# Gram matrices and decays of the delta rule split off from the block substitution, in a Trainium2 kernel for one hybrid decoder layer

## The chip, the cores and the metric

The kernel runs on one core of one Trainium2 chip. The metric is the time of one execution on the device in microseconds (us), the median of the runs. In what follows PE is TensorE's matmul, PEld its weight load, DVE is VectorE, ACT is ScalarE, POOL is GpSimd, and SP is SyncE, which issues all of the kernel's DMAs. All of the core's engines take their instructions in the order in which they were written.

## What is computed

2048 tokens of width 1024, with 16 meta tokens ahead of them, go through one layer and a last RMSNorm. The reference, cut to what matters here:

```python
h = rmsnorm(x, norm_g)
p = h @ w_in                                  # 1024 x 8208
qkv, dn_z, dn_a, dn_b, sc_b, sc_c, sc_h, sc_z = split(p)
q, k, v = split(silu(causal_dwconv(qkv, width 4)))    # 8 heads x 128; q, k L2-normalised
g    = -exp(A_log) * softplus(dn_a + dt_bias);  beta = sigmoid(dn_b)
# gated delta rule, by chunks
g      = cumsum(g)
decay  = exp(where(causal, g_i - g_j, -inf))
a_low  = where(strict, beta * (k k^T) * decay, 0)
u, w   = solve(I + a_low, [v * beta, k * beta * exp(g)])
qk     = (q k^T) * decay
for each chunk:  v_new = u - w S;  o = (q exp(g)) S + qk v_new;  S = S exp(g_last) + k_dec^T v_new
o_dn = rmsnorm(o) * silu(dn_z)
o_sc = sc_b * causal_dwconv(sc_c * sc_h, width 3) * silu(sc_z)
out  = rmsnorm(x + concat(o_dn, o_sc) @ w_out)
```

## The kernel before

The tokens go in two halves of 1024. In the first phase each half runs 64 jobs, a job being the projection of one tile of 128 channels (`Job`, `run_group`): 3 groups of tokens by 24 matmuls, since each product is made of three float32r products of split operands (`hh`, `hl` are the high and low parts of the tokens, `wh`, `wl` those of the weights `wr`). Eight jobs belong to a head. Within a head they come as q, k, c, h, b, the gate sz of the short convolution, v, z, but for the first head of the first half and the last two of the second. Job j's weights are loaded by `load_w` into one of two `wr` buffers and split by ACT (`wh`) and DVE (`wl`). The second phase is the output projection, 48 matmuls a unit, and needs nothing of the last head until its eighth token tile.

The order of all engines but SP is written by the program itself. `Model` (line 30) follows the engines with costs of its own; the projections are cut into pieces of two or three matmuls, and after each piece `pump` (line 234) lets each of some streams (Python generators) take a step when the model's time has come to what it yielded. `require` (line 251) stops the projections, and lets only the streams go on, until a step is done: a head's k job waits for the scan of the head two before (`pre_k`, line 825), its v job for the transposes of the head before (`pre_v`, line 837, key `vr`).

The delta rule of the sixteen heads (8 heads, 2 halves) is four such streams, each going through the heads in order:

- `delta_front` (line 971): for head i the decays `E` (loaded as `gtd` rows, subtracted, masked by POOL, exp by ACT), then in four pieces the split keys and queries `kp` and six matmuls (the Gram matrices, `ta<-nb` in the profile, since `kp` takes the place of tile `nb`), which DVE turns into `M` (written over `E`) and `P`. The diagonal 32 x 32 blocks of `M` go to DRAM and back as `nb` (`nbd<-E`, `nb<-nbd`). On the first half `meta_inputs` handles the meta tokens. Then `substitution` inverts the blocks: 31 times a product (`prod<-nb,XT`) and a sum (`XT<-prod`) on DVE, row by row; `prod` starts as a copy of the constant `eyep`, made by POOL. The result goes to DRAM (`xtd<-XT`).
- `delta_back` (line 1108): the blocks come back as `W` (`W<-xtd`); six groups of four transposes bring k, v and q to token order (`ta<-ident,k` and so on); then `(I + M)^-1` of the whole chunks by small matmuls, the first of them `ta<-X,E`.
- `delta_scan` (line 1288): eight steps, one a chunk, each a chain PE `rec<-S,k`, DVE `yy`, PE `rec<-yy,W`, ACT `vn`, PE `rec<-vn,kd`, DVE `S`.
- `delta_out` (line 1338): norm, gate and store.

So `delta_front` starts the Gram pieces of head i + 1 only after the substitution of head i. The Gram pieces, `nb` and the prologue share the tile `nb`; the gate values use the tile `gw`. `normalize` (line 536) prepares the second half's tokens in between.

Of the kernel before, what the change touches and what calls it, by code (L numbers as in the profile page):

```python
# [12 lines left out]
ALU = mybir.AluOpType  # L13
# [16 lines left out]
class Model:  # L30
    """Time of each engine and of each tile, as work is issued; it decides the order of issue only."""
# [32 lines left out]
    def after(self, *aps, slot=None, eng=None, lag=0.0, least=0.02):  # L64
        """Time until the tiles are written, the slot is free and the engine is through but for lag."""
        t = self.free["PE"] + least
        for a in aps:
            t = max(t, self.ready.get(a.tensor.name, 0.0))
        if slot is not None:
            q = self.slots.get((id(slot[0]), slot[1]), ())  # L70
            if len(q) == self.bufs.get((id(slot[0]), slot[1])):
                t = max(t, self.used.get(q[0], 0.0))
        if eng is not None:
            t = max(t, self.free[eng] - lag)
        return t - self.free["PE"]
# [86 lines left out]
class Recorded:  # L162
    """The engines of a core, with all that they are given entered into the model."""
# [10 lines left out]
def hybrid_trunk(  # L174
# [41 lines left out]
    # ---- order of emission: a stream of projections, cut into pieces, and streams of dependent  # L216
    # steps that are issued between the pieces. `model` follows the engines as they are given work;
    # a step yields the time until what its successor needs is there.
# [28 lines left out]
    def when_done(fn, ap, most=100.0):  # L247
        """Issue fn once ap has been written."""
        timed.append((clk() + min(after(ap), most), fn))
# [46 lines left out]
    def newton(dst, a, y, t):  # L296
        """dst = y (1.5 - 0.5 a y^2): one Newton step for a ** -0.5 from y."""
        nc.vector.tensor_tensor(out=t, in0=y, in1=y, op=ALU.mult)
        nc.vector.scalar_tensor_tensor(t, t, -0.5, a, op0=ALU.mult, op1=ALU.mult)
        nc.vector.scalar_tensor_tensor(dst, t, 1.5, y, op0=ALU.add, op1=ALU.mult)  # L300
# [16 lines left out]
    # ---- constants of the first phase  # L317
# [12 lines left out]
    # eyep[32 q + block, m, i] = (i == 8 q + m)  # L330
    eyep = vt(pp, [128, 8, 32], "eyep")
# [10 lines left out]
    def constants():  # L342
        prow = vt(vp, [128, 128], "yy")
        nc.sync.dma_start(prow[0:96], dn_conv_w[0].rearrange("j (t p) -> (j t) p", p=128))
        nc.sync.dma_start(prow[96:120], sc_conv_w[0].rearrange("j (t p) -> (j t) p", p=128))
        nc.sync.dma_start(prow[120:121], dn_out_g)
        nc.sync.dma_start(negA, dn_A_log.partition_broadcast(128).rearrange("p o h -> p (o h)"))
        nc.sync.dma_start(dtb, dn_dt_bias.partition_broadcast(128).rearrange("p o h -> p (o h)"))
        wabr = vt(vp, [128, 128], "vn").rearrange("p (k c) -> p k c", c=16)
        nc.sync.dma_start(wabr, win[:, :, 4096:4112])  # L350
        while ("prologue", 0) not in done:
            yield 0.2
        yield after(prow, slot=(pta, "ta"))
        yield from hold()
        pt = ptile(pta, "ta", [128, 512])
        tr(pt[:, :121], prow[:121], 121)
        nc.vector.tensor_copy(pcol[:, :121], pt[:, :121])
        nc.gpsimd.memset(triu, 1.0)
        nc.gpsimd.affine_select(
            out=triu,  # L360
            in_=triu,
            pattern=[[1, 128]],
            compare_op=ALU.is_ge,
            fill=0.0,
            base=0,
            channel_multiplier=-1,
        )
        nc.gpsimd.memset(qcar, 0.0)
        nc.gpsimd.memset(ucar, 0.0)
        nc.gpsimd.memset(W, 0.0)  # L370
        nc.gpsimd.memset(X[0:64], 0.0)
        nc.gpsimd.memset(eyep, 0.0)
        for q in range(4):
            for m in range(8):
                nc.gpsimd.memset(eyep[32 * q : 32 * q + 32, m, 8 * q + m : 8 * q + m + 1], 1.0)
        nc.scalar.activation(negA, negA, AF.Exp)
        nc.vector.tensor_scalar(negA, negA, -1.0, None, op0=ALU.mult)
        nc.scalar.activation(wab[:, :, 0:16], wabr, AF.Copy)
        nc.vector.tensor_tensor(out=wab[:, :, 16:32], in0=wabr, in1=wab[:, :, 0:16], op=ALU.subtract)
        done.add("constants")  # L380
# [8 lines left out]
    def turn(hf, xt, k0, i, col, n, g):  # L389
        """Channels 4 k0 .. 4 k0 + 3 of a token tile into h^T."""  # L390
# [18 lines left out]
    def statistics(xt, n, jk):  # L409
        """mean square + eps and its approximate power -0.5."""  # L410
        ms, y = vt(vp, [128, 1], "pxm", bufs=3)[:n], vt(vp, [128, 1], "pxy", bufs=3)[:n]
        nc.scalar.activation(jk[:n, :D], xt, AF.Square, accum_out=ms)
        nc.gpsimd.tensor_scalar(ms, ms, 1.0 / D, EPS, op0=ALU.mult, op1=ALU.add)
        power(y, ms, 1, n)
        return ms, y

    def rootmean(xt, n):
        """(mean square + eps) ** -0.5 by ACT and GpSimd."""
# [14 lines left out]
    def prologue0():  # L433
        """h^T = (RMSNorm(x))^T of the first half as float32r parts hi + lo, [channel, k, token]
        by group."""
# [100 lines left out]
    def normalize(i):  # L536
        """RMSNorm of token tile i of the second half, to DRAM until the first half is through."""
        xt = vt(dp, [128, NC, 128], "kd").rearrange("p c i -> p (c i)")
        nc.sync.dma_start(xt, xs[HALF + 128 * i :][:128])
        yield after(xt)  # L540
        st = statistics(xt, 128, vt(dp, [128, 1840], "gw", dt=BF16))
# [48 lines left out]
    def hold(tag="ta", keep=False):  # L590
        """Wait until no step holds tag over several yields; or hold it."""
        while tag in held:
            yield 0.2
        if keep:
            held.add(tag)
# [3 lines left out]
    def gates(hf):  # L599
        """Token-major gate values [128, head, chunk]; on half 0 chunk 8 holds the meta tokens."""  # L600
# [21 lines left out]
        gw = vt(dp, [128, 920], "gw")  # L622
# [24 lines left out]
        # e = exp(-|a|), exp(-|b|), exp(min(b, 0))  # L647
# [11 lines left out]
        # log1p(e) = 2 atanh(s), s = e / (2 + e) <= 1 / 3  # L659
# [34 lines left out]
        nc.sync.dma_start(ged[hf, :Wd], gT[:Wd])  # L694
        G[hf] = dict(beta=beta, gcum=gcum, neg=neg, nch=nch)
# [3 lines left out]
    # ---- projections  # L699
# [76 lines left out]
    def conv_job(hf, s, col, t, pre, emit):  # L776
        """Projection, causal width-4 convolution and SiLU of channel tile t of q | k | v."""
# [43 lines left out]
    def slot_jobs(hf, s):  # L821
# [51 lines left out]
        # short convolution of channel tile s  # L873
# [67 lines left out]
    # ---- gated delta rule  # L941
    def substitution(nb, XT, prod):
        """Rows of (I + N)^-1 of unit lower triangular 32 x 32 blocks, a block and 8 columns per
        partition; nb[j, i] = N[i, j], XT[col, i], prod[col, i] = identity on entry."""
# [9 lines left out]
    def decay(hf, row0, n, E, gc):  # L954
        """E[j, c, i] = exp(g_i - g_j) for i >= j, else 0."""
# [14 lines left out]

    def delta_front():
        """Decays, the two triangular matrices, and the inverses of the diagonal blocks."""
        for i in range(2 * NH):
# [14 lines left out]
            )  # L988
            if hf == 0:
                Em = vt(dp, [NM, 1, NM], "mE")  # L990
# [20 lines left out]
            for c2 in range(4):  # L1011
                c0 = 2 * c2
                yield after(slot=(dp, "nb"))
                kp = vt(dp, [128, 2, 2, 2, 128], "nb", dt=F32R)
# [11 lines left out]
                for c in range(2):  # L1026
# [4 lines left out]
                    mmr(o_, lhsT=l_[:, :128], rhs=h_, start=False, stop=True)  # L1031
                yield after(pm, E)
# [27 lines left out]
            # inverses of the 32 x 32 diagonal blocks: partition 32 q + 8 b + c, columns 8 q .. 8 q + 7  # L1060
# [8 lines left out]
            if hf == 0:  # L1069
                yield from meta_inputs(hd, g_, d, Em)  # L1070
            yield after(nb)
# [12 lines left out]
            nc.gpsimd.tensor_copy(prod, eyep)  # L1084
# [20 lines left out]
            half[i] = dict(M=M, P=P, cd=cd, ir=ir, cj=cj)  # L1105
            done.add(("front", i))

    def delta_back():
        """The inverses of the whole chunks, and what the scan needs by token."""
        for i in range(2 * NH):  # L1110
# [11 lines left out]
            # q exp(g); token-major k, q norms, v  # L1122
# [41 lines left out]
            # (I + M)^-1 of the whole chunks from the blocks'  # L1164
# [52 lines left out]
    def meta_inputs(hd, g_, d, Em):  # L1217
        """The meta tokens' chunk: all but the inverse of its block."""
# [35 lines left out]
        def rows():  # L1254
            """One column of (I + N)^-1 per partition; entry 0 brings in the identity."""
# [82 lines left out]
    def delta_out():  # L1338
        """Norm, gate and store of the outputs."""
# [45 lines left out]
    # ---- output projection: weights of one column half as hi + lo parts, k by k  # L1385
# [9 lines left out]
    def first_wo():  # L1395
        """The first column half, into the place of the token groups that are through."""
# [28 lines left out]
    def load_mix(u, h):  # L1425
        """Half h of the mixed channels of unit u's tokens, in two float32r parts."""
# [18 lines left out]
    def unit_mm(u, nxt, same=None):  # L1445
        """One token tile by one column half; with `same`, the next unit takes over the mix."""
# [24 lines left out]
    # ---- first phase: all projections, the delta rule beside them  # L1471
# [21 lines left out]
    start(delta_front())  # L1493
    start(delta_back())
# [24 lines left out]
    # ---- second phase: output projection, residual, final norm  # L1519
# [117 lines left out]
```

## Time and profile before

| | |
|---|---|
| median of 3 runs | 2257.49 us (2250.55 to 2260.83) |
| span of the profiled execution, first to last instruction | 2248.0 us |
| its own time, by the median of the runs | some 9.5 us around the span |
| PE busy | 2175.4 us, 97% |
| DVE busy | 1456.6 us, 65% |
| ACT busy | 864.9 us, 38% |
| POOL busy | 153.3 us, 7% |
| mean granted clock of TensorE | 0.991 |

The execution that was profiled has no time listed of its own; its span and the 9.5 us to the median stand for it. The profile's page gives busy time by engine; the waits say which engine waited for what; the windows cut the span into stretches; the timelines list single instructions; the chain follows back from the last instruction to what released each. Matmuls overlap one another, so it is the time from start to start that tells the pace.

### The profile page before, as it was taken

To read this page: it belongs to the slowest core of one execution; us is meant where nothing else is said; L and a number is where in the kernel's file an instruction comes from. 1 tells how busy PE (TensorE), PEld (TensorE's weight loads), DVE (VectorE), ACT (ScalarE), POOL (GpSimd) and SP (SyncE) were. 2 spreads that over 40 slices of the span, in tenths; PEclk is the share of its full clock that TensorE was granted. 3 is DMA by queue.
4 is the path that set the end of the run, shared out by engine and by line. 5 is a ranking of instruction groups with operands and counts; after the bars stand their busy time and mean duration, and the time that the engine had idled before them with its cause. 6 is when DMAs were issued, how large, how long until landed. Compare 5 with 4: busy or idle time off the path is not lost.

```text
span 2248.0 us, 38710 instructions
## 1 busy us (share of the span) xinstructions
PE 2175.4 (97%) x15024; PEld 2061.8 (92%) x15024; DVE 1456.6 (65%) x4031; ACT 864.9 (38%) x2080; POOL 153.3 (7%) x312
## 2 busy tenths in 40 slices
PE   6999999999999999999999999999998799999998
PEld 6999999999999998999999999999998798888886
DVE  4676867676767767776868677676766465544322
ACT  5534434444444333443434343525352324422111
POOL 4000100000000000101000000000000000000000
PEclk9999999999999999999999999999999899999999
DMA  6444345443535677524343544253546664645321
GB/s 140 75 81 70 84 68 91 67 93 67 92 67 104 82 83 60 134 43 80 52 83 57 78 52 83 48 88 43 88 49 60 53 94 139 222 164 189 119 94 57
DMA packets 257237, 196.46 MB, mean 87 GB/s; under 512 B 62085, under 2 KB 226446, under 8 KB 257054
## 3 DMA queue, kind: packets, MB, share of 16 engines
q1 hardware_dynamic: 257054, 194.00, 47.5%
q8 instruction: 118, 1.93, 0.4%
q14 instruction: 65, 0.53, 0.1%
HBM read 157.89 MB, written 36.06 MB: 86 GB/s over the span
## 4 chain that ended last, share of the span: by engine, by line
PE 87%; DMA 6%; DVE 4%; SPq 1%; ACT 1%; issue 1%; POOL 0%; POOLq 0%; DVEq 0%; ACTq 0%
PE mm L118 74%; PE ta L118 7%; PE rec L118 4%; PE o L118 2%; SPq L118 1%; DMA nb<-nbd 1%; DMA wr<-in_w_in_dram 1%; DMA kd<-in_x_dram 1%; DVE prod L118 1%; DMA xtd<-XT 1%; DMA W<-xtd 1%; ACT junk L118 1%; DVE acc L118 1%; DVE XT L118 1%; DMA nbd<-E 0%
## 5 line engine op out<-in xcount | busy, mean ns | idle before, releaser
L118 PE MATMUL mm<-hh,wh 128*128 128x384 f32 (+3 forms) x3328 | 1043.6, 335 | 6.4 <-ACT hh L118 5.3
L118 PE MATMUL mm<-hl,wh 128*128 128x384 f32 (+3 forms) x3328 | 1015.1, 326 | 0.0
L118 PEld LDWEIGHTS mm<-hh,wh 128*128 128x128 f32 x3328 | 626.8, 189 | 21.0 <-ACT hh L118 5.9
L118 PEld LDWEIGHTS mm<-hl,wh 128*128 128x128 f32 x3328 | 627.3, 189 | 9.7
L118 PE MATMUL mm<-hh,wl 128*128 128x384 f32 (+3 forms) x3200 | 622.6, 327 | 2.8 <-DVE wl L118 2.8
L118 PEld LDWEIGHTS mm<-hh,wl 128*128 128x128 f32 x3200 | 512.6, 189 | 9.9 <-DVE wl L118 3.2
L118 DVE TENSOR_TENSOR wl<-wr,wh 128x512 fp32r<-128x512 f32 x348 | 233.8, 691 | 98.8 <-ACT wh L118 67.0
L118 DVE SCALAR_TENSOR_TENSOR acc<-raw,pcol,acc 128x384 f32<-128x384 f32 (+2 forms) x432 | 245.5, 573 | 60.5 <-ACT acc L118 55.9
L118 ACT ACTIVATE wh<-wr 128x1024 fp32r<-128x1024 f32 x178 | 187.8, 1055 | 79.3 <-PE mm L118 44.5
L118 DVE SCALAR_TENSOR_TENSOR prod<-nb,XT 128x8 f32<-128x8 f32 (+30 forms) x496 | 192.8, 389 | 39.1 <-DMA nb<-nbd 34.0
L118 DVE TENSOR_REDUCE XT<-prod 128x8 f32<-128x16 f32 (+30 forms) x496 | 147.2, 297 | 17.0
L118 ACT ACTIVATE raw<-mm 128x272 f32<-128x272 f32 (+2 forms) x144 | 65.7, 456 | 214.1 <-PE mm L118 214.1
L118 ACT ACTIVATE vn<-rec,cj 128x128 f32<-128x128 f32 x128 | 46.9, 366 | 252.0 <-PE rec L118 246.7
L118 ACT ACTIVATE sc_c<-mm 128x384 f32<-128x384 f32 (+4 forms) x99 | 45.0, 456 | 161.8 <-PE mm L118 158.0
L118 PE MATMUL mm<-oh,wh 128*128 128x512 f32 x256 | 101.9, 398 | 0.0
L118 PE MATMUL mm<-ol,wh 128*128 128x512 f32 x256 | 100.3, 392 | 0.0
L118 DVE TENSOR_TENSOR y<-mm,y 128x512 f32<-128x512 f32 x23 | 15.9, 692 | 110.7 <-PE mm L118 110.7
L118 DVE SCALAR_TENSOR_TENSOR yy<-rec,neg,vr 128x128 f32<-128x128 f32 x128 | 44.4, 347 | 62.3 <-PE rec L118 61.8
L118 ACT ACTIVATE ojk<-y 128x512 bf16<-128x512 f32 x23 | 14.5, 631 | 182.6 <-DVE y L118 127.0
L118 ACT ACTIVATE acc<-mm,pcol 128x272 f32<-128x272 f32 (+2 forms) x144 | 78.2, 543 | 0.0
L118 DVE SCALAR_TENSOR_TENSOR S<-S,egl,rec 128x128 f32<-128x128 f32 x104 | 35.8, 344 | 59.2 <-PE rec L118 58.3
L118 POOL TENSOR_TENSOR opy<-mo,nhalf 128x4 f32<-128x4 f32 x32 | 35.3, 1102 | 544.0 <-DVE mo L118 507.3
(244 smaller groups left out, 2548.8 us busy)
## 6 DMA issues: line engine op xcount, KB each, us to landing
wr<-in_w_in_dram SPq DMA_DIRECT2D x128, 512.0 KB, 9.0
wr<-mixd SPq DMA_DIRECT2D x50, 512.0 KB, 4.5
E<-gtd SPq DMA_DIRECT2D x16, 512.0 KB, 4.1
qd<-ged SPq DMA_DIRECT2D x16, 512.0 KB, 8.4
nb<-nbd SPq DMA_DIRECT2D x64, 128.0 KB, 5.3
mixd<-zs SPq DMA_DIRECT2D x32, 256.0 KB, 3.2
out_dram<-y SPq DMA_DIRECT2D x16, 512.0 KB, 2.6
mixd<-sc_y SPq DMA_DIRECT2D x32, 192.0 KB, 2.4
```

Source lines behind the costliest of these rows:

```text
L118: r = real(*args, **kw)
```

## The change

`delta_front` becomes two streams. The new `delta_front` makes decays and Gram pieces and ends with `done.add(("gram", i))`; the new `delta_inverse` waits for that, loads `nb`, and does the rest. The split keys `kp` move from tile `nb` to the gate values' tile `gw`, which grows from 920 to 1024 columns; `gates` and `normalize` now take turns on it with the Gram pieces through `hold("gw")`. Before the decays of a head of the first half, the front waits for the step ("meta", i - 1), since the tile `mE` has one buffer. The constant `eyep` goes: POOL makes the identity anew for each head, one memset and four `affine_select`.

```diff
 def delta_front():
     for i in range(2 * NH):
...
+            Em = None
             if hf == 0:
+                while i and ("meta", i - 1) not in done:
+                    yield 0.3
                 Em = vt(dp, [NM, 1, NM], "mE")
...
             for c2 in range(4):
                 c0 = 2 * c2
-                yield after(slot=(dp, "nb"))
-                kp = vt(dp, [128, 2, 2, 2, 128], "nb", dt=F32R)
+                yield after(slot=(dp, "gw"))
+                yield from hold("gw", True)
+                kp = vt(dp, [128, 2, 2, 2, 128], "gw", dt=F32R)
...
                     mmr(o_, lhsT=l_[:, :128], rhs=h_, start=False, stop=True)
+                held.discard("gw")
...
+            fronts[i] = (M, Em)
+            half[i] = dict(M=M, P=P, cd=cd, ir=ir, cj=cj)
+            done.add(("gram", i))
+
+    def delta_inverse():
+
+        for i in range(2 * NH):
+            hf, hd = divmod(i, NH)
+            while ("gram", i) not in done:
+                yield 0.3
+            d, g_ = slot[i], G[hf]
+            M, Em = fronts[i]
             nb = vt(dp, [128, 32, 32], "nb")
...
             if hf == 0:
                 yield from meta_inputs(hd, g_, d, Em)
+            done.add(("meta", i))
             yield after(nb)
...
-            nc.gpsimd.tensor_copy(prod, eyep)
+            nc.gpsimd.memset(prod, 1.0)
+            for q in range(4):
+                nc.gpsimd.affine_select(
+                    out=prod[32 * q : 32 * q + 32],
+                    in_=prod[32 * q : 32 * q + 32],
+                    pattern=[[-1, 8], [1, 32]],
+                    compare_op=ALU.is_equal,
+                    fill=0.0,
+                    base=-8 * q,
+                    channel_multiplier=0,
+                )
...
-            half[i] = dict(M=M, P=P, cd=cd, ir=ir, cj=cj)
             done.add(("front", i))
...
     start(delta_front())
+    start(delta_inverse())
     start(delta_back())
```

In `gates`, `gw` is taken with `hold("gw", True)` and given back at the end; in `constants`, `eyep` with its 33 memsets is left out.

Where instructions come to stand. First PE, in the first half, around the token-order transposes of head 0 and the start of head 1's v job (`mm<-hh_..,wh 128x272`). Before, the six groups of transposes stood apart among the projections of the jobs ahead; the last of them stood here:

```order
L118 MATMUL mm<-hh_281,wl 128x384 x8
L118 MATMUL mm<-hh_428,wh 128x384
L118 MATMUL mm<-hl_429,wh 128x384
L118 MATMUL ta<-ident,q 128x128 x4
L118 MATMUL mm<-hh_428,wh 128x384
```

Now (`ta<-mkv,mXT` and `ta<-mvn,mkv` are the meta tokens' two products):

```order
L118 MATMUL mm<-hh_427,wl 128x384 x8
L118 MATMUL ta<-mkv,mXT 16x128
L118 MATMUL ta<-mvn,mkv 128x128
L118 MATMUL ta<-ident,k 128x128 x4
L118 MATMUL ta<-ident,vT 128x128 x4
L118 MATMUL ta<-ident,q 128x128 x4
L118 MATMUL ta<-ident,k 128x128 x4
L118 MATMUL ta<-ident,vT 128x128 x4
L118 MATMUL ta<-ident,q 128x128 x4
L118 MATMUL mm<-hh_188,wh 128x272
```

All 26 stand in one piece between the last matmul of one job and the first of the next, with no projection among them.

Second PE again, at the start of head 2's k job, around the last steps of head 0's scan (the first `mm` row of 128x272 is that job's). Before:

```order
L118 MATMUL rec<-S,k 128x128
L118 MATMUL o<-S,qd 128x128
L118 MATMUL mm<-hh_428,wh 128x384
L118 MATMUL mm<-hl_429,wh 128x384
L118 MATMUL mm<-hh_428,wh 128x384
L118 MATMUL mm<-hl_429,wh 128x384
L118 MATMUL mm<-hh_428,wl 128x384 x4
L118 MATMUL rec<-yy,W 128x128
L118 MATMUL mm<-hh_428,wl 128x384 x4
L118 MATMUL rec<-vn,kd 128x128
L118 MATMUL o<-vn,P 128x128
L118 MATMUL mm<-hh_189,wh 128x272
```

Now, the job before ending in the `x2` row:

```order
L118 MATMUL mm<-hh_427,wl 128x384 x4
L118 MATMUL rec<-ident,os 128x128 x4
L118 MATMUL mm<-hh_427,wl 128x384 x2
L118 MATMUL rec<-yy,W 128x128
L118 MATMUL rec<-vn,kd 128x128
L118 MATMUL o<-vn,P 128x128
L118 MATMUL rec<-S,k 128x128
L118 MATMUL o<-S,qd 128x128
```

After these come eight more of the same chain (`rec<-yy,W`, `rec<-vn,kd`, `o<-vn,P`, `rec<-S,k`, `o<-S,qd`, `rec<-yy,W`, `rec<-vn,kd`, `o<-vn,P`) and only then `mm<-hh_188,wh 128x272`: thirteen chained products with no projection between. The same thirteen stand in one piece at the start of head 6's k job, where before the scan of head 4 had ended 74 projection matmuls earlier.

Third SP, near the end of the first phase, around the blocks of head 14. Before:

```order
L118 DMA mixd<-sc_y 128x3x128
L118 DMA xtd<-XT 32x8x32 x4
L118 DMA mixd<-sc_y 128x3x128
L118 DMA wr<-in_w_in_dram 128x8x128
L118 DMA W<-xtd 32x8x32 x4
```

Now:

```order
L118 DMA mixd<-sc_y 128x3x128
L118 DMA xtd<-XT 32x8x32 x4
L118 DMA mixd<-sc_y 128x3x128
L118 DMA W<-xtd 32x8x32 x4
L118 DMA wr<-in_w_in_dram 128x8x128 x2
```

The load of a job's weights that stood ahead of `W<-xtd` stands behind it.

## Rows read from the trace of the kernel before

**Rows 1.** Page, part 1: busy time by engine over the whole span

```profile
PE 2175.4 (97%) x15024; PEld 2061.8 (92%) x15024; DVE 1456.6 (65%) x4031; ACT 864.9 (38%) x2080; POOL 153.3 (7%) x312
```

**Rows 2.** Waits of PE: waited for, us in total, times, longest

```profile
PE ta L118 <- issue: 15.0, 3, 13.6
PE rec L118 <- DVE os L118: 10.5, 5, 6.4
PE rec L118 <- DVE S L118: 7.4, 3, 3.5
```

**Rows 3.** Windows: stretch, length, busy PE to POOL, PEclk, DMA share, GB/s

```profile
1700.00:1705.00 5.00, 0.00 (x0) 0.00 (x0) 2.19 (x10) 0.00 (x0) 1.31 (x3) 0.81 0.33 88
1705.00:1710.00 5.00, 4.04 (x14) 4.05 (x15) 4.30 (x13) 0.00 (x0) 0.00 (x0) 0.50 0.18 52
...
1900.00:1950.00 50.00, 50.00 (x249) 42.02 (x248) 21.63 (x44) 18.86 (x42) 2.30 (x2) 1.00 0.49 161
```

**Rows 4.** Timeline of PE after the wait at 1700: start us, us, instruction

```profile
1708.15 0.52 PE L118 MATMUL mm<-hh,wh 128*128 128x384 f32 x1
1708.47 0.52 PE L118 MATMUL mm<-hl,wh 128*128 128x384 f32 x1
...
1710.03 0.33 PE L118 MATMUL mm<-hh,wh 128*128 128x384 f32 x1
1710.20 0.33 PE L118 MATMUL mm<-hl,wh 128*128 128x384 f32 x1
```

**Rows 5.** Chain of waits, head 14's blocks to DRAM and back

```profile
1749.46 9.91 DMA xtd<-XT
1759.56 13.12 DMA W<-xtd
```

**Rows 6.** Timeline of SP, the weight load between those two

```profile
1756.41 0.39 SPq L118 DMA_DIRECT2D wr<-in_w_in_dram  x1
```

**Rows 7.** DMA issues: count, KB each, median us from issue to landing

```profile
xtd<-XT SPq DMA_DIRECT2D x64, 32.0 KB, 4.5
W<-xtd SPq DMA_DIRECT2D x64, 32.0 KB, 1.9
```

**Rows 8.** Waits of DVE for the blocks of the substitution

```profile
DVE prod L118 <- DMA nb<-nbd: 34.0, 10, 8.7
```

**Rows 9.** Timeline of PE, head 6's scan behind such a wait

```profile
803.12 0.49 PE L118 MATMUL rec<-S,k 128*128 128x128 f32 x2 [2.25 <-DVE S L118]
```

**Rows 10.** Groups by line: busy us, mean ns of one, idle before

```profile
L118 DVE SCALAR_TENSOR_TENSOR acc<-raw,pcol,acc 128x384 f32<-128x384 f32 (+2 forms) x432 | 245.5, 573 | 60.5 <-ACT acc L118 55.9
L118 DVE TENSOR_TENSOR wl<-wr,wh 128x512 fp32r<-128x512 f32 x348 | 233.8, 691 | 98.8 <-ACT wh L118 67.0 <-PE mm L118 31.5
L118 DVE SCALAR_TENSOR_TENSOR prod<-nb,XT 128x8 f32<-128x8 f32 (+30 forms) x496 | 192.8, 389 | 39.1 <-DMA nb<-nbd 34.0 <-issue 2.4
L118 ACT ACTIVATE wh<-wr 128x1024 fp32r<-128x1024 f32 x178 | 187.8, 1055 | 79.3 <-PE mm L118 44.5 <-DMA wr<-in_w_in_dram 16.0 <-issue 12.0
L118 DVE TENSOR_REDUCE XT<-prod 128x8 f32<-128x16 f32 (+30 forms) x496 | 147.2, 297 | 17.0
...
L118 ACT ACTIVATE vn<-rec,cj 128x128 f32<-128x128 f32 x128 | 46.9, 366 | 252.0 <-PE rec L118 246.7 <-PE mm L118 5.2
...
L118 DVE SCALAR_TENSOR_TENSOR S<-S,egl,rec 128x128 f32<-128x128 f32 x104 | 35.8, 344 | 59.2 <-PE rec L118 58.3
```

**Rows 11.** Timeline of PE, first and last of head 14's six transpose groups

```profile
1748.41 0.60 PE L118 MATMUL ta<-ident,k 128*128 128x128 f32 x4
...
1753.80 0.60 PE L118 MATMUL ta<-ident,q 128*128 128x128 f32 x4
```

**Rows 12.** Groups by line on POOL, the small mask of the meta tokens

```profile
L118 POOL TENSOR_SCALAR_AFFINE_SELECT mE<-mE 16x16 f32<-16x16 f32 x8 | 3.0, 369 | 1.1 <-DVE mE L118 1.1
```

**Rows 13.** Timeline of POOL, the mask of head 8's decays

```profile
1015.13 1.10 POOL L118 TENSOR_SCALAR_AFFINE_SELECT E<-E 128x1024 f32<-128x1024 f32 x1 [62.15 <-DVE sq L118]
```

**Rows 14.** Timeline of DVE at that time

```profile
1015.30 1.47 DVE L118 TENSOR_TENSOR wl<-wr,wh 128x512 fp32r<-128x512 f32 x1
```

More of the change, by code (lines that the diff above doesn't have):

```diff
@@ L329, in hybrid_trunk @@
     triu = vt(pp, [128, 128], "triu")
-    eyep = vt(pp, [128, 8, 32], "eyep")
     W = vt(pp, [128, NC, 128], "W")
@@ L371, in constants @@
         nc.gpsimd.memset(X[0:64], 0.0)
[L372 to L375, printed above, removed]
         nc.scalar.activation(negA, negA, AF.Exp)
@@ L540, in normalize @@
         yield after(xt)
+        yield from hold("gw")
         st = statistics(xt, 128, vt(dp, [128, 1840], "gw", dt=BF16))
@@ L621, in gates @@
         pt = ptile(pta, "ta", [128, 512])
-        gw = vt(dp, [128, 920], "gw")
+        yield from hold("gw", True)
+        gw = vt(dp, [128, 1024], "gw")
         ab2 = gw[:, 0:288].rearrange("p (c m) -> p c m", m=32)
@@ L969, in hybrid_trunk @@
     half = {}
+    fronts = {}
     def delta_front():
@@ L1012, in delta_front @@
                 c0 = 2 * c2
-                yield after(slot=(dp, "nb"))
-                kp = vt(dp, [128, 2, 2, 2, 128], "nb", dt=F32R)
+                yield after(slot=(dp, "gw"))
+                yield from hold("gw", True)
+                kp = vt(dp, [128, 2, 2, 2, 128], "gw", dt=F32R)
                 kh, kl = kp[:, 0], kp[:, 1]
@@ L1031, in delta_front @@
                     mmr(o_, lhsT=l_[:, :128], rhs=h_, start=False, stop=True)
+                held.discard("gw")
                 yield after(pm, E)
```

## The prediction

> **What bounds the kernel.** I read the page's busy times first: PE is busy for 97% of the span, DVE for 65% [rows 1]. The reader should conclude that the end moves only if PE's work changes, or if the time in which PE stands still does. PE's work does not change: the edit adds and removes no matmul. The output projection, where PE is busy all of the time [rows 3], can neither gain nor lose. So I read PE's waits next. The three that matter here are one of 13.6 us, which hides under "issue" in a total of 15.0; the wait for `os`, 6.4 at the longest; and the wait for a scan's `S`, 7.4 in three pieces [rows 2]. The rest are single microseconds or belong to the start. A wait costs a little more than its length: in the 5 us after the 6.4 us wait the granted clock is 0.50, TensorE's level of 1.2 GHz [rows 3], and matmuls of 384 columns start 0.32 us apart there, against 0.17 from 1710 on [rows 4]. PE is busy for 4.04 us of that stretch, at half pace; 2 us are lost.
>
> What stands behind them is DMA. The 13.6 us are head 14's blocks on their way back: `xtd` takes 9.9 us, `W` 13.1 [rows 5], where the medians are 4.5 and 1.9 [rows 7], because a load of 512 KB was issued on the same queue between the two [rows 6]. The waits for `os` and `S` are DVE's: DVE stands for `nb`, 34.0 us in all, 8.7 at the longest [rows 8], and what PE needs is queued behind on DVE, as in head 6's scan, 2.25 us [rows 9].
>
> **The change part by part.** *The order of PE.* The Gram pieces of the next head now share DVE with the substitution of this one. The first half's heads finish it later (head 0's last row stands some 100 projection matmuls later in the order), and three `require`s are now met late. There PE gets pieces with no projection in them, and must go through their chain at the chain's pace.
>
> First, head 1's v job waits for head 0's transposes: two meta products and six groups stand in one piece. In head 14 six such groups took from 1748.41 to 1754.4, 6.0 us [rows 11], spread among projections and not hurried. Ahead of them ACT has a `wh` of 1.06 us [rows 10] and two small copies, together some 2. So 8 us pass, of which PE's own work is 26 small matmuls, some 2.8. Idle: 5. Bounds: 3 (nothing ahead) to 8.
>
> Second, head 2's k job waits for head 0's scan: thirteen chained products in one piece. DVE works in order, and between the piece's start and its last `yy` the order has on DVE five `acc`, two `wl`, six pairs of `prod` and `XT`, two `S` and two `yy` (like `S`): 5 x 0.573 + 2 x 0.691 + 6 x 0.686 + 4 x 0.344 = 9.7 us [rows 10], and three small rows of the meta tokens, 0.6. Rows on DVE overlap by a little; I take 9.5. Then come one product, `vn` of 0.37 [rows 10] and the last two, some 1.3. Of these 11 us PE's own work is about 3. Idle: 8. Lower bound: the chain alone, two and two thirds steps of `S`, `yy`, `vn` (1.05) and three products (0.8), 5 us, idle 2. Upper: 10.
>
> Third, the same at head 6's k job, for head 4's scan: four `acc`, one `wl`, four pairs, two `S`, two `yy`, 2.3 + 0.7 + 2.7 + 1.4 = 7.1 us, meta rows 0.5, the tail 1.3, less 3 of PE's own and a little overlap. Idle: 6.5, bounds 2 and 9.
>
> That makes 19.5 us. For the clock after each I take the 2 us found above, three times, 6 us; below, nothing, if the small products keep it up; above, 9. Head 0's first block product stands so soon behind its transposes that `W` may be late: 2 us, bounds 0 and 5. New idle time: 27.5 us, bounds 7 and 41.
>
> *The order of SP.* For head 14 the weight load now stands behind `W`. With `xtd` still behind an earlier load, I take 10 us off the 13.6, bounds 0 and 13.6 (16 with the clock). The load that now goes out later is due two jobs on, and is hidden by the job between. What is late next is head 15's `nb`, whose order stays.
>
> *`nb` no longer shared.* On the first half the blocks now land 12 to 28 us of PE's work ahead of the substitution (all heads but head 0), so DVE's waits for `nb` end there: 2.3 us of PE [rows 9]. On the second half the order leaves the same 18 or so projection matmuls as before between them, 3 us, and each `nb` still has a load or `qd` ahead of it on SP; the 6.4 and 3.5 us of [rows 2] stay. Bounds: from 10 us gained with their clock to 5 lost.
>
> *POOL.* One copy a head becomes a memset and four masks. By the nearest row, a small mask of 0.37 us [rows 12], that is some 1.7 us a head. POOL is busy 7% and waits for nothing but the tile, so it runs ahead while DVE stands for `nb`; cover: that wait. If it is gone (the first half), DVE waits up to 1.3 us a head. I take 0 for PE, 5 above. DVE can also be held while POOL works: beside a mask of 1.10 us [rows 13] a `wl` took 1.47 us [rows 14], against a mean of 0.69 [rows 10]. The Trainium skill ("SBUF — State Buffer", section "SBUF: two separate sides") gives the reason, a port pair that one of the two engines holds for a whole instruction, when DVE reads two operands from SBUF and GpSimd reads SBUF; the trace agrees with these two rows. By that rule the 64 masks would add, as an estimate, up to 24 us to DVE's work if all of them fell beside such reads, and a few microseconds to the sum. I leave it at 0, since most of DVE's delays so far did not reach PE.
>
> *No cost.* `constants` loses 33 memsets on POOL; nobody waits for them. The new `hold("gw")` and ("meta", i - 1) only delay steps that are otherwise early. Head 15 ends earlier, but the output projection does not wait for it.
>
> **The sum.** 27.5 - 10 - 2.3 = 15 us more. The profiled execution, 2248.0 us of span, would have 2263, and the median of 2257.5, which lies 9.5 above the span, 2272.5; I say 2272. About 0.5%, 11 us, is what a measurement of this kernel can tell from no change.
>
> **The rivals.** *They cancel.* The pieces cost their lower bounds (7 to 15 us in all), and `W` loses its whole wait with the clock (16 and 2.3): 2246 to 2262, or no change. For: the savings have measured sizes, the costs are worked out. Against: DVE's list in the second piece is long and can't be skipped. With the part of my own range under 2269 I give no change 0.37.
>
> *Faster, by the DMA queue.* Every wait of the second half behind a DMA goes: not `W` alone (16 with its clock) but also the `nb` waits (6.4 and 3.5 and their clock, 13), and 2.3 and 3 of small ones. Place: SP from head 13 on; it decides if `nb` of heads 14 and 15 lands over 5 us earlier. 34 saved, 19 paid (half of the clock, no late `W`): 2242. For: head 15's front comes some 10 us earlier in the order. Against: the order on SP around head 14's `nb` is the same as before. Chance 0.10.
>
> *The savings do not come.* `W` of head 14 or of another head meets a load as before, and POOL holds DVE: 27.5 - 2 + 5 = 30 us, 2288. For: the distance from the last row of a substitution to its first block product shrinks a little for most heads (head 14: 14.6 to 14.1 us of PE's work), so other heads come nearer to a wait. Chance 0.18.
>
> *It moves too little.* On the second half q and k of a head come just ahead of its Gram pieces, and the substitutions stand within some 15 us of their old places. If that held for the first half too, the time would be 2257 less the 12 of `W`, 2245; but the order of PE shows that it does not. I give it 0.03, as a part of the 0.10.
>
> **How the numbers follow.** My forecast, 2262 to 2282, has 0.47, of which 0.12 lies under 2269. Slower by over 0.5% is then 0.35 + 0.18 = 0.53; no change 0.25 + 0.12 = 0.37; faster 0.10. The range runs from 2246 (the cancelling case's low end) to 2290 (the case without savings), and leaves out about 0.1 on each side.
>
> **What would show it.** Right: PE's waits have three new stretches in the first half, at about 210, 260 and 700 us, with 13 or 26 small matmuls in single file, 5 to 9 us idle in each, and a granted clock near 0.5 in parts; the wait before `ta<-X,E` of head 14 falls from 13.6 to under 5 us; DVE's wait for `nb` on the first half is gone. Wrong: if these stretches pass without idle time of 10 us in all, the chain is shorter than I made it; if the end moves while PE's idle time does not, the bound is not what I say.

## The result, and the profile after

The changed kernel takes 2283.07 us, the median of four runs (2277.27 to 2286.07), beside 2255.09 for the kernel before: a ratio of 1.0115 (95% interval 1.0091 to 1.014). It is slower by over 0.5%, and inside the range of the prediction, 11 us above its forecast: 28 us more than before, where 15 were forecast. The profiled span is 2275.5 us, 27.5 more than before.

The page of the changed kernel, part 1, against [rows 1]:

```profile
PE 2192.7 (96%) x15024; PEld 2071.2 (91%) x15024; DVE 1463.7 (64%) x4027; ACT 863.8 (38%) x2078; POOL 186.7 (8%) x343
```

The number of matmuls is the same, but PE is busy for 17.3 us more. The span less PE's busy time is what PE stands: 72.6 us before, 82.8 now. So 10 of the 27.5 us are standing, and 17 are the same matmuls taking longer.

The waits of PE in the changed kernel (waited for, us in total, times, longest), against [rows 2]:

```profile
PE mm L118 <- DVE wl L118: 6.9, 6, 4.0
...
PE mm L118 <- issue: 6.7, 1, 6.7
PE rec L118 <- ACT vn L118: 6.5, 8, 2.1
PE rec L118 <- DVE os L118: 6.4, 3, 5.3
PE rec L118 <- DVE S L118: 5.8, 4, 3.6
PE ta L118 <- ACT gw L118: 5.1, 2, 3.8
...
PE ta L118 <- DVE gw L118: 3.6, 2, 1.9
```

The 13.6 us before head 14's `ta<-X,E` are gone: that row of the timeline has no idle time now. New are the waits for `vn`, a link of the scan's chain; those for `gw`, where a Gram piece waits for its split keys; and 6.7 us under "issue", which is of another kind (last section).

The timeline of PE in the changed kernel, head 0's transposes ahead of head 1's v job (start us, us, instruction, idle before and its releaser):

```profile
206.31 0.39 PE L118 MATMUL ta<-mkv,mXT 16*16 16x128 f32 x2
208.06 0.48 PE L118 MATMUL ta<-mvn,mkv 16*128 16x128 f32 x2 [1.36 <-ACT mvn L118]
...
210.36 1.12 PE L118 MATMUL ta<-ident,q 128*128 128x128 f32 x4 [0.80 <-ACT kd L118]
...
213.14 1.12 PE L118 MATMUL ta<-ident,vT 128*128 128x128 f32 x4 [0.81 <-ACT junk L118]
...
214.94 0.57 PE L118 MATMUL mm<-hh,wh 128*128 128x272 f32 x1
...
260.95 0.38 PE L118 MATMUL rec<-yy,W 128*128 128x128 f32 x2
263.46 0.49 PE L118 MATMUL rec<-vn,kd 128*128 128x128 f32 x2 [2.13 <-ACT vn L118]
...
270.22 0.80 PE L118 MATMUL rec<-S,k 128*128 128x128 f32 x2 [1.22 <-DVE S L118]
270.81 0.64 PE L118 MATMUL o<-S,qd 128*128 128x128 f32 x2
271.45 0.80 PE L118 MATMUL rec<-yy,W 128*128 128x128 f32 x2
...
273.64 0.57 PE L118 MATMUL mm<-hh,wh 128*128 128x272 f32 x1
```

From 260.95 on the same view shows head 0's scan ahead of head 2's k job, thirteen products in single file, 12.7 us long. A `rec` row takes 0.38 us at the start of the piece and 0.80 from 270 on: most of the chain itself runs at half pace. In the windows (stretch, length, busy PE to POOL, PEclk, DMA share, GB/s):

```profile
206.00:220.00 14.00, 11.04 (x63) 9.34 (x61) 6.08 (x12) 7.76 (x30) 0.00 (x0) 0.76 0.58 121
260.00:275.00 15.00, 9.54 (x40) 7.65 (x40) 14.20 (x43) 4.81 (x12) 0.00 (x0) 0.64 0.35 67
275.00:280.00 5.00, 5.00 (x28) 5.00 (x28) 4.48 (x11) 2.11 (x10) 1.25 (x1) 0.72 0.64 170
725.00:736.00 11.00, 6.87 (x29) 5.12 (x27) 10.57 (x34) 3.93 (x9) 0.00 (x0) 0.65 0.22 66
736.00:750.00 14.00, 14.00 (x86) 13.96 (x86) 9.70 (x26) 4.99 (x15) 2.09 (x4) 0.91 0.44 80
```

The granted clock is a mean between the 2.4 GHz level (1.00) and the 1.2 GHz level (0.50). It is 0.64 in the second piece though PE counts as busy for 9.54 of 15 us there, and 0.72 in the 5 us behind it, where PE does not stand at all.

The start of the same projection matmul in both traces tells where the time goes (the small `wab` products of the gates are not counted). Number 800 of the first phase starts 1.0 us later than before, number 1600 21.8 us later (354.2 against 332.4), number 4800 37.8 us later (1024.2 against 986.4). At the end 27.5 remain. So all is lost in the first half, and some 10 us come back in the second, around the place where the 13.6 us lay.

### The profile page after: what moved, and what is told of

Same layout as the page of the kernel before. It is cut to its first block, busy times and chain, and to the rows that moved or that the text cites. A ratio compares the mean times of both kernels' runs of the same rounds, so it can differ in the third digit from the quotient of the medians.

```text
span 2275.5 us, 38771 instructions
## 1 busy us (share of the span) xinstructions
PE 2192.7 (96%) x15024; PEld 2071.2 (91%) x15024; DVE 1463.7 (64%) x4027; ACT 863.8 (38%) x2078; POOL 186.7 (8%) x343
## 3 DMA queue, kind: packets, MB, share of 16 engines
q8 instruction: 118, 1.93, 0.3%
## 5 line engine op out<-in xcount | busy, mean ns | idle before, releaser
L118 PEld LDWEIGHTS mm<-hh,wh 128*128 128x128 f32 x3328 | 630.4, 190 | 21.6 <-ACT hh L118 5.4
L118 DVE TENSOR_TENSOR wl<-wr,wh 128x512 fp32r<-128x512 f32 x344 | 231.7, 694 | 100.9 <-ACT wh L118 58.8
L118 DVE SCALAR_TENSOR_TENSOR prod<-nb,XT 128x8 f32<-128x8 f32 (+30 forms) x496 | 190.1, 383 | 24.4 <-DMA nb<-nbd 20.9
```

Source lines behind the costliest of these rows:

```text
L118: r = real(*args, **kw)
```

## The experiments

Three readings were to be told apart: that the masks on POOL cost something; that the head start itself puts dependent work together on PE; and that any other disturbance of the planner's order would have done the same, because the old order was an unusually good one. An order that the planner writes is called a draw in what follows. "Standing" below is span less PE's busy time, both from each run's page.

**The masks alone, the order of PE left as it was (`masks_quiet`).** Kernel before, with the memset and four masks in place of the copy; the planner is told the copy's cost.

```diff
-            nc.gpsimd.tensor_copy(prod, eyep)
+            tc.nc.gpsimd.memset(prod, 1.0)
+            for q in range(4):
+                tc.nc.gpsimd.affine_select(
...
+            model.issue("POOL", 0.12 + 256 / 300.0, [prod], [eyep])
```

> The kernel before, with the memset and the four masks on POOL in place of the copy, and the planner told the copy's cost, so that PE's order is the old one, row for row. Theory 'order' (the loss comes from where the pieces of the chains stand on PE): no change, ratio 0.997 to 1.003 (2248 to 2262 us), no new stretch of idle time on PE. Rival 'POOL' (the masks hold DVE, and the late identity holds the substitution): 64 masks cost 10 us or more, ratio 1.005 to 1.012, and the rows of the substitution are longer on DVE or start later after nb has landed.

Measured: 2254.98 us, ratio 0.9998 (0.9985 to 1.001). Its groups by line (busy us, mean ns, idle before), against [rows 10]:

```profile
L118 DVE TENSOR_TENSOR wl<-wr,wh 128x512 fp32r<-128x512 f32 x348 | 233.8, 691 | 99.5 <-ACT wh L118 69.5 <-PE mm L118 29.7
L118 DVE SCALAR_TENSOR_TENSOR prod<-nb,XT 128x8 f32<-128x8 f32 (+30 forms) x496 | 192.5, 388 | 39.2 <-DMA nb<-nbd 36.6
```

Both means are those of before, 691 and 389 (now 388), with POOL busy for 186.5 us instead of 153.3. The masks cost nothing that these runs can tell, which is some 3 us. This run also shows how well a profile repeats: with the same order PE is busy for 2179.7 us, 4.3 more than before.

**No head start, all else of the change (`serial_all_quiet`, `serial_all`).** The front of a head waits for the substitution of the head before; in the first of the two the planner is also told the copy's cost for the masks.

```diff
+            while i and ("front", i - 1) not in done:
+                yield 0.3
```

> The changed kernel, but front i + 1 waits for front i to be through, as before, and the planner is told the copy's cost for the masks: what is left of the change is the split keys' place and the masks themselves. Its order has one piece without a projection, of ten products near the end of the first half. Theory 'order': the loss goes, ratio 0.997 to 1.004; head 14's W still stands behind a load and waits some 13 us; DVE's waits for nb on the first half fall as in the changed kernel. Rival 'POOL and place': ratio 1.006 or more, without any long piece of chained products.

> As serial_all_quiet, but the planner sees what it takes the masks to cost (some 2 us a head, before each substitution). In its order two pieces without a projection come back: five products at head 2's k job, eight at head 6's. Theory 'order': each product of such a piece costs about 0.8 us more than among projections (13 took 12.7 us in the changed kernel), so 4 and 6 us and some clock, 10 to 14 us above serial_all_quiet, if head 14's W waits as long there: 2258 to 2272 us, less up to 14 if that wait goes. Rival (the pieces cost little, the loss is spread): within 4 us of serial_all_quiet.

Measured: 2277.71 us, 1.0103 (1.0078 to 1.0129), and 2282.89 us, 1.0124 (1.0107 to 1.014). Both are slow without the head start. The waits of PE, of the first:

```profile
PE ta L118 <- issue: 13.1, 3, 11.7
PE ta L118 <- DVE X L118: 9.6, 4, 7.3
PE o L118 <- ACT os L118: 8.9, 8, 1.6
...
PE rec L118 <- DVE os L118: 7.0, 1, 7.0
PE rec L118 <- DVE yy L118: 6.2, 1, 6.2
```

The 11.7 is head 14's `W` again, with the load ahead of it. The rest stands elsewhere than in either kernel: 7.3 us at `ta<-X,E` of another head, 6.2 us in a scan, 8.9 us in small bits. The theory that the head start by itself makes the 28 us falls here, though these two still keep the split keys in `gw`, which was not tried by itself. In `serial_all` a piece of 5 and one of 8 dependent products stand in PE's order, though no head start is there.

**The wait for head 14's `W` alone (`before_w14`).** In the kernel before, one 512 KB load of weights is held back until behind `W`, by a one-column copy on POOL that reads `W`. The load that the edit names (`J.col` 6032, the 124th) is not the one of [rows 6] but the one before it, which stood ahead of `xtd`. SP's timeline of the kernel before:

```profile
1742.34 0.37 SPq L118 DMA_DIRECT2D wr<-in_w_in_dram  x1
```

The 125th, that of [rows 6], came to stand behind `W` with it, since the planner's order moved.

```diff
+            if (J.hf, J.col) == (1, 6032) and not behind:
+                late.append(j)
+                return
             J.wr = vt(wp, [128, KT, 128], "wr")
+            if behind:
+                nc.gpsimd.tensor_copy(J.wr[:, 0, 0:1], W[:, 0, 0:1])
...
+            if late and i == 14:
+                load_w(late.pop(), True)
```

> The kernel before, with the one weight load that stood between head 14's xtd and W put behind W (a POOL copy of one column of W into the buffer holds the load back). Theory 'order': the 13.6 us wait falls to under 2 us, and the time falls by 13 to 17 us with the clock: 2239 to 2244 us, ratio 0.992 to 0.995. Rival (the late load is the next wait): the wait moves to the wl or wh of the job two on, or to head 15's nb or W, and the ratio is 0.997 to 1.0.

Measured: 2248.69 us, 0.997 (0.9959 to 0.998), the fastest of all kernels here. SP's timeline (start us, us, instruction), and PE's waits from 1700 to 2000 us:

```profile
1751.70 1.82 SPq L118 DMA_DIRECT2D xtd<-XT  x4
1754.83 1.78 SPq L118 DMA_DIRECT2D W<-xtd  x4
1757.87 1.02 SPq L118 DMA_DIRECT2D wr<-in_w_in_dram  x2
```

```profile
PE rec L118 <- DVE os L118: 6.7, 1, 6.7
PE rec L118 <- DVE S L118: 4.8, 1, 4.8
PE mm L118 <- ACT hl L118: 2.5, 1, 2.5
PE mm L118 <- DVE wl L118: 1.7, 2, 1.3
PE mm L118 <- ACT wh L118: 1.5, 2, 1.2
```

`xtd` now takes 1.7 us instead of 9.9, `W` is there 4.2 us after its first issue where 13.1 stood, and the 13.6 us wait is gone. Some 7.5 us of it reach the end. From matmul 8600 to the last projection of the first phase this trace gains 13.3 us on the one before, and in the output projection it loses 7.1 of them again. Head 15's `nb` lands no earlier: DVE goes on with it at 1821.8 us (1821.6 before), and PE's wait for `S` behind it is 4.8 us (3.5 before). In the output projection PE waits 1.3, 2.5 and 1.2 us for its operands (at 1863.3, 1871.5 and 1964.6 us), where one wait of 1.7 stood.

**One number of the planner, and nothing else (`redraw_before_a`, `redraw_before_b`, `redraw_after_a`, `redraw_after_b`).** Both kernels are drawn anew with the same two edits. No part of the computation changes; only the order that the planner writes moves.

```diff
-    LATENCY = 0.17
+    LATENCY = 0.18
```

in the two that end in `a`, and in the two that end in `b`

```diff
-    LAG = 0.5
+    LAG = 0.55
```

> The kernel before with one number of the planner changed, its latency between engines 0.18 for 0.17 us. No instruction is added or removed; only the order that the planner writes is drawn anew. Theory 'split' (the streams of their own cost 25 to 30 us by themselves): the order before is one of many as good, so 2250 to 2264 us. Theory 'draw' (the order before is a lucky draw of the planner, and whatever disturbs the planner costs about 1%, as the two serial kernels do): 2268 to 2290 us. Both together: this kernel 2262 to 2275, and the changed kernel drawn anew still some 10 to 20 us above it.

> The changed kernel with the same one number, 0.18 for 0.17. Its order has pieces without a projection of 26, 26 and 7 products (the changed kernel: 26, 13 and 13). Theory 'split': 2280 to 2298 us, with PE's waits inside the two long pieces. Theory 'draw': as far from the kernel before as its twin, 2265 to 2285, no matter how long the pieces are.

> The kernel before with another number of the planner changed, the lag of DVE up to which side work is issued, 0.55 for 0.5 us; an order drawn anew, with pieces of 7 and 13 products that the order before does not have. Theory 'split': 2250 to 2268 us (the pieces at some 0.7 us for each product). Theory 'draw': 2265 to 2285 us.

> The changed kernel with 0.55 for 0.5; pieces of 26, 13 and 7 products. Theory 'split': 2272 to 2290 us, 15 us or more above redraw_before_b. Theory 'draw': within 8 us of redraw_before_b.

Measured: the kernel before 2301.57 us (1.0193, 1.0164 to 1.0221) and 2269.25 us (1.0057, 1.0037 to 1.0077); the changed kernel 2286.98 us (1.0148, 1.0122 to 1.0174) and 2280.58 us (1.0105, 1.0085 to 1.0125). The waits of PE in `redraw_before_a`, the slowest of all:

```profile
PE ta L118 <- DVE X L118: 13.2, 5, 8.9
PE rec L118 <- DVE yy L118: 11.0, 3, 8.0
PE rec L118 <- DVE S L118: 9.7, 5, 4.0
PE o L118 <- ACT os L118: 8.9, 6, 1.8
```

Against [rows 2] the wait of 13.6 has gone, three others have come or grown (for `X` 3.8 before, for `os` 1.3, for `yy` none), and that for `S` is 9.7 instead of 7.4. Its PE trace has only one piece without a projection that lasts over 2.5 us, five products of a scan (1112.2 to 1115.5 us): long pieces are not what makes it slow. A hundredth of a microsecond in a planner's number costs 45 us; the change that was to be judged costs 28.

**Four more draws (`second_a`, `second_b`, `full_c`, `before_pick`).** The first two have the head start on the second half alone, `full_c` is the whole change, `before_pick` the kernel before, each with other planner numbers.

```diff
+            while 0 < i < NH and ("front", i - 1) not in done:
+                yield 0.3
```

holds the front back on the first half in the `second` pair. `second_a`: `STEP` 1.2, `LAG` 0.7, `BACKLOG` 5, and the copy's cost for the masks. `second_b`: `STEP` 1.1, `LATENCY` 0.15, `BACKLOG` 4. `full_c`: `LATENCY` 0.15, `SUBST` 0.9, `META` 8, the copy's cost. `before_pick`: `LAG` 0.6, `BACKLOG` 4, `META` 8. These numbers were chosen for orders that looked good beforehand, so the four are no blind draws.

> The changed kernel with the head start on the second half alone (on the first half front i + 1 waits for front i), the planner told the copy's cost for the masks, and three of its numbers drawn anew (STEP 1.2, LAG 0.7, BACKLOG 5). Its order has one piece without a projection, of ten products. Theory 'split': on the first half the head start costs some 20 us or more in every drawing, by its long pieces, and on the second half it saves head 14's W wait of 13 us; here the first half has almost none of these pieces, so 2240 to 2256 us. Theory 'draw' (one drawing is as good as the other, and only the order before is lucky): 2270 to 2295 us, as the other kernels drawn anew.

> The same, with the planner's own cost of the masks, and other numbers (STEP 1.1, LATENCY 0.15, BACKLOG 4); its order has no piece without a projection at all. Theory 'split': 2240 to 2258 us. Theory 'draw': 2270 to 2295 us. Head 14's W stands behind a load that goes out between the parts of xtd, so some of that wait may be left.

> The changed kernel with its head start on both halves, and numbers of the planner chosen for an order with fewer pieces (LATENCY 0.15, SUBST 0.9, META 8, the copy's cost for the masks): one piece of 21 products at head 2's k job, three of four. Theory 'split': the pieces of the first half can be moved but not avoided, so 2262 to 2278 us, still slower than the kernel before. Rival (with the right numbers the full change is as good as any): 2240 to 2257 us.

> The control for the two kernels above: the kernel before, without any part of the change, with its planner's numbers chosen in the same way (LAG 0.6, BACKLOG 4, META 8); one piece of five products and three of four. If the choice of numbers alone makes the gain, this one is as fast as second_a, 2240 to 2256 us. If the head start on the second half adds to it, it stays at 2252 to 2268 us, with the waits for W and nb at heads 13 to 15.

Measured, with all the others (each ratio is to the kernel before as it ran beside that kernel, 2255.09 to 2256.91 us):

| kernel | us | ratio (95%) | PE busy | standing | matmul 800 to 1600, against before |
|---|---|---|---|---|---|
| before | 2255.09 | 1 | 2175.4 | 72.6 | 0 |
| masks_quiet | 2254.98 | 0.9998 (0.9985-1.001) | 2179.7 | 74.4 | -0.1 |
| before_w14 | 2248.69 | 0.997 (0.9959-0.998) | 2180.4 | 65.6 | 0.0 |
| *head start on the first half* | | | | | |
| the change | 2283.07 | 1.0115 (1.0091-1.014) | 2192.7 | 82.8 | +20.9 |
| redraw_after_a | 2286.98 | 1.0148 (1.0122-1.0174) | 2200.0 | 85.0 | +28.7 |
| redraw_after_b | 2280.58 | 1.0105 (1.0085-1.0125) | 2193.9 | 86.2 | +21.6 |
| full_c | 2300.72 | 1.0186 (1.016-1.0212) | 2199.0 | 100.9 | +20.0 |
| *drawn anew, no head start on the first half* | | | | | |
| redraw_before_a | 2301.57 | 1.0193 (1.0164-1.0221) | 2193.8 | 98.2 | -3.1 |
| redraw_before_b | 2269.25 | 1.0057 (1.0037-1.0077) | 2182.9 | 80.9 | +1.1 |
| before_pick | 2277.42 | 1.0085 (1.0062-1.0107) | 2190.1 | 86.8 | +3.4 |
| serial_all_quiet | 2277.71 | 1.0103 (1.0078-1.0129) | 2187.8 | 87.4 | -6.6 |
| serial_all | 2282.89 | 1.0124 (1.0107-1.014) | 2192.4 | 87.4 | +0.8 |
| second_a | 2273.64 | 1.0065 (1.0043-1.0088) | 2191.4 | 80.7 | +7.9 |
| second_b | 2254.91 | 0.9989 (0.9978-1.0) | 2179.7 | 73.4 | +0.1 |

The last column is the time from the start of the 800th projection matmul to that of the 1600th, less the 161.7 us of the kernel before; heads 0 and 1 are worked on there. By the end times the two families overlap (2281 to 2301, and 2255 to 2302). By this column they do not: 20.0 to 28.7 us with the head start on the first half, -6.6 to 7.9 without. The column follows the pieces without a projection: in the four, those over 2.5 us in this stretch add up to 21.3, 31.3, 21.2 and 17.6 us (in the order of the table), in the seven to 9.1 (`second_a`), 4.5 (`redraw_before_b`), 3.8 (`before_pick`), 3.4 (`serial_all`) and nothing in the other three. Some of it is paid back soon: at matmul 2400 the four are behind by 15.5, 25.4, 20.8 and 21.5 us, a mean of 20.8, and the seven by a mean of 6.9 (-1.2 to 11.5). So the head start on the first half costs some 14 us at its place in the mean of these draws, and all four lie above all seven. No expectation had named this stretch beforehand, and further on the families overlap again: at matmul 4800 the four are behind by 37.8 to 49.0 us, the seven by 13.2 to 47.4.

Much of the rest goes with the draw. The seven kernels without that head start have a mean of 2276.8 us, some 21 above the kernel before, and one of them only comes back to its time; the four with it have 2287.8. How much of the 28 us at the end is the one and how much the other stays open, since single draws differ by up to 47 us.

Of the ranges set beforehand, `serial_all`, `redraw_before_a`, `full_c` and `before_pick` came out slower than any. `serial_all_quiet` fell into the range of 'POOL and place', though POOL's part is nothing by `masks_quiet`. `before_w14` came out as its rival had it, `second_a` as 'draw' and `second_b` as 'split'; `redraw_after_b`, 11 us above its twin, lies between the two. Neither theory holds alone.

## Why the prediction was right or wrong, point by point

**The number.** The range was met because it is 44 us wide. Of the change itself, 15 us were forecast and 28 measured, which is nearer to the rival without savings (2288), though the saving at `W` came whole. Terms that were too large (idle time of the pieces) and waits that no term had stand against each other in it; to that extent the hit is luck. Three of the sums do not come out as written either: the third piece gives 5.9 us and not 6.5, the 19 "paid" in the faster rival is 22.5 by its own terms, and the cancelling case reaches 2254 at its upper end, not 2262.

**The pieces: places right, idle time less, cost about right.** They came at 206, 261 and 725 us (forecast 210, 260, 700). By their rows PE stands 3.0, 5.5 and 4.1 us in them, 12.6 in all, where I had 5, 8 and 6.5, and nothing under the lower bounds; two of the three are under the 5 to 9 that I gave as the sign of being right. What I took for PE's own work, 3 us in each piece of thirteen, is some 7, since the products stand in single file and most run at half pace: from 260.95 to 273.64 are 12.7 us, of which 7.2 are products. Among projections they would have taken some 2.6, an estimate at 0.2 us each (0.14 to 0.22 us from start to start in head 0's scan around 240 us). So the second piece costs 10 us, as much as my 8 of idle time and 2 of clock, but in other shares.

**The clock: the term that was mis-sized.** I had three times 2 us, read off one wait of the kernel before [rows 3, 4]. PE's busy time grew by 17.3 us, or 13.0 against the repeat with the old order. The step that failed is "for the clock after each I take the 2 us": the clock is lost in the pieces too, and behind other waits than these three: the granted clock is 0.64 in the 5 us behind the waits for `gw` of head 6 (776 to 781 us), and 0.50 from 883 to 888 us, around the last of head 7's. In the seven kernels of the table that were drawn anew without the head start the busy time, too, is mostly higher where the standing is, so this is not peculiar to the change.

**Head 0's `W`: 2 us forecast, none measured.** The first block product behind it has no idle time.

**Head 14's `W`: direction right, 10 forecast.** It lost its whole 13.6 us. The place of the weight loads on SP was the cause: `before_w14`, which has the two of them behind `W`, loses the wait as well. It also shows that only 7.5 us of such a wait reach the end. I had named head 15's `nb` as what is late next and put no price on it.

**`nb`: right.** DVE's waits in the changed kernel, against [rows 8]:

```profile
DVE prod L118 <- DMA nb<-nbd: 20.9, 5, 9.0
```

The four longest that are left, 2.6, 9.0, 6.9 and 2.1 us, belong to heads 13, 14, 15 and 9; on the first half 0.4 us are left, and the 2.25 us of [rows 9] are gone. The waits for `os` and `S` on the second half stayed (5.3 and 3.6 now, 6.4 and 3.5 before).

**POOL: 0, right.** By the rule of the Trainium skill ("SBUF — State Buffer", section "SBUF: two separate sides"), 64 masks more could have held DVE's reads. `masks_quiet` has the masks and neither a longer `wl` nor a later end; what the rule says was seen only in the two single rows [rows 13, 14].

**What was in no term.** Waits for split keys, `ta<-gw`, 8.7 us; longer waits for `wl`, 6.9 against 2.8; the 6.7 us under "issue". That is 19.5 us. With the terms above, 12.6 - 13.6 - 2.3 + 19.5 = 16.2 us more standing, where the page has 10.2; the 6 us between are other rows that rose or fell, most of all `rec` for `os` (10.5 to 6.4) and `ta<-X` (3.8 to 0.2). Of the waits for `wl`, 5.5 us stand in the output projection, at 1901.6 and 1971.0 us, which the prediction held to "neither gain nor lose" (one of 1.7 there before). I had counted the move to `gw` as one that only delays early steps; for heads 6 and 7 the split keys came late for PE. Whether `hold("gw")` or the load on ACT and DVE made them late was not tried.

**The step behind all of these.** I compared the change with one order and took that order for the neutral case. It is a good draw: of seven others without the head start on the first half, six are slower by 0.57 to 1.93%. The rival "the order as such" was missing from the prediction; with it, I would have given slower more than 0.53. The cancelling case, the rival I gave 0.37, had the pieces at 7 to 15 us in all; their idle time of 12.6 lies in that, and `W`'s wait went as it said. It fell by the lower pace of PE and by the waits that no term had.

**What would be kept.** `before_w14` beats both kernels, by 0.3% and 1.4%. `second_b` equals the kernel before. No version with the head start on the first half comes near.

## What to carry to other kernels

Where a planner writes the order, compare a change with several redraws of the old kernel, made by moving one of the planner's numbers a little, before the change is praised or blamed. Read the order for pieces of dependent small products with no independent matmul between, and price such a piece by its whole length, here 12.7 us for thirteen, not by its idle time alone; but an order without long pieces can be slow too. A wait that is removed is worth what is left after the next late thing: here 7.5 us of 13.6.

## What the runs showed of the hardware that was not expected

PE stood for 6.7 us at 933 us in the changed kernel with nothing that the profile shows to wait for. Its timeline and two windows:

```profile
932.72 0.39 PE L118 MATMUL o<-S,qd 128*128 128x128 f32 x2
939.80 0.48 PE L118 MATMUL mm<-hh,wh 128*128 128x384 f32 x1 [6.69 <-issue]
```

```profile
925.00:933.00 8.00, 8.00 (x109) 7.07 (x108) 1.56 (x6) 2.43 (x5) 0.00 (x0) 1.00 0.98 91
933.00:940.00 7.00, 0.31 (x2) 0.23 (x2) 0.28 (x1) 0.00 (x0) 0.00 (x0) 0.76 0.50 131
```

The DMA engines were busy for 0.98 of the 8 us ahead. The queue that brings instructions, by the DMA view of three stretches, moved this from 880 to 912 us, nothing at all from 912 to 936, and this from 936 to 944 (packets, MB, share):

```profile
q8 instruction: 2, 0.03, 0.4%
...
q8 instruction: 2, 0.03, 1.5%
```

That PE's next instructions came late behind the data is what these rows suggest; it was seen in this kernel alone and not tried by an experiment. The Trainium skill ("Runtime: NRT & Kernel Launch", section "Instruction fetch mechanics") says that an engine fetches its instructions in blocks of 16 KiB over a queue of its own, and that crossing a block costs one DMA step, "mostly hidden". The blocks of 16 KB agree (two packets, 0.03 MB); if the reading is right, the step was not hidden here, at 6.7 us.

In the second piece the chained products of 128 columns soon run at half pace, 0.80 us a row instead of 0.38, while PE counts as busy for 64% of the stretch (9.54 of 15 us, granted clock 0.64): a busy share does not tell the pace.
